# A float32 decoder block on one core: attention's gate products, the w_out loads and two operand sums placed anew

## The chip, the cores and the metric

The kernel runs on one core of a Trainium2 chip. The time of a kernel is the device time of one execution in microseconds (us). The kernel before took 751.6 us (median of three runs, 751.37 to 751.66). The engines are named as the profile does: PE (TensorE, matrix products), PEld (its weight loads), DVE (VectorE), ACT (ScalarE), POOL (GpSimd), SP (the engine that issues most transfers).

## The reference

One layer of a decoder, 1024 tokens with 16 meta tokens ahead of them, model width 1024. Everything is float32.

```python
h = rmsnorm(x, norm_g)
u_pool, z_pool, q, k, v, z_attn, f_logit, g_pool, g_attn = split(h @ w_in)
y_pool = causal_multiscale_pool(u_pool, pool_w, pool_scale) * silu(z_pool)   # 4 groups, windows 2, 4, 8, 16
log_f  = log_sigmoid(f_logit + b_forget)
y_attn = forgetting_attention(q, k, v, log_f) * silu(z_attn)                  # 8 heads of 64, causal softmax
merged = sigmoid(g_pool) * (y_pool @ w_up_pool) + sigmoid(g_attn) * (y_attn @ w_up_attn)
out    = rmsnorm(x + merged @ w_out, final_norm_g)                            # meta tokens dropped
```

## The kernel before, in words

**Split operands.** Each float32 operand of a product is rounded to a high part by ACT (for example `whi`, `yh`, line 133 or 727) and a low part is formed as the difference (`wlo`, `yl`, `oph`, `opy`). A product is then three matrix products: high by high, high by low, low by high (`g_mm3`, line 140). The low part of a w_in weight is made by POOL in four pieces of 256 columns (`pool_tt`, line 117, called at line 134); that of the pooling branch (`yl`, line 728) is made by POOL too; those of the up-projection's weights (line 811), of attention's output (line 760) and of the last product's operands (line 914) are made by DVE.

**The stages.** Norm and first projections; attention with the other projections filled in between (to about 502 us); then the part that the change touches:

1. *The za projections* (four weights, `left[0]` to `left[3]`, 502 to 575 us). `za[p]` is silu of a projection (line 741). Between them stand the pooling branch's group maps (`pooled(g)`, line 800, 12 matrix products for two groups), the normalisation of attention's output (`attn_norm`, line 748) and the gate, `Y[p] = Y[p] * za[p]` (`attn_gate`, line 750). `half_raw` runs a projection's first half and one matrix product of its second; `run` does the rest. For p = 0 and 1 the gate runs on POOL in eight pieces, for p = 2 and 3 on DVE.
2. *Sixteen up-projections* (`up`, line 819, 5.6 us each, 575.55 to 665.08). The order is the list `steps` (line 943). Each takes a raw weight (`rawu`) and a gate row (`rl`) from SP's queue. Attention's output is wanted from the fifth on. Step n of the loop (line 946) also issues a load of one block row of w_out (`w_load`, line 894) from n = 4 to 11, and with each second one the first sums on it (`t_first`, line 923, on POOL).
3. *The output product* by seven products of half size, 10.9 us each (`prod`, line 985), from sums of blocks: with G the merged branches and W = w_out, S1 = G21 + G22, S2 = S1 - G11, S3 = G11 - G21, S4 = G12 - S2, and T1 to T4 of W in the same way. They are computed in place, so S2 lies in G11, S4 in G12, T4 in W21. `prep(n)` rounds and splits the operand pair of product n, one ahead of the product. The operand sets lie in two buffers, `opy` for even n and `oph` for odd n. The operands are, in turn, (G11, W11), (G12, W21), (S2, T2), (S1, T1), (S3, T3), (S4, W22), (G22, T4). P6 in the title of the change is the product of S2 and T2, the third.

PE's order is written out by hand. On the other engines a scheduler orders the instructions by its own model of time, with the program's order as a start; `after(ins, prev)` (line 100) makes it place `ins` behind `prev` without a semaphore. Each engine and each queue then runs in that order. A buffer of the tag `b` (gate rows, za, the pooling branch) is handed on in the order in which it is let go in the program.

Of the kernel before, what the change touches and what calls it, by code (L numbers as in the profile page):

```python
# [11 lines left out]
ALU = mybir.AluOpType  # L12
# [31 lines left out]
def r32(ap):  # L44
    return ap.bitcast(F32)
# [7 lines left out]
def tile_hybrid_block(ctx, tc, x, meta, norm_g, w_in, b_forget, pool_w, pool_scale,  # L53
                      w_up_pool, w_up_attn, w_out, final_g, out):
    nc = tc.nc
# [44 lines left out]
    def after(ins, prev):  # L100
        tc.add_manual_dep(ins.ins, prev.ins.name,
                          mybir.DependencyInfo(mybir.DependencyClass.NoSync, mybir.DependencyReason.DATA),
                          reason="order")

    def rstd_of(ss):
        n = ss.shape[0]
        r = sm.tile([128, 1], F32, name="rstd", bufs=4)
        nc.vector.tensor_scalar(r[:n], ss, EPS, None, op0=ALU.add)
        nc.gpsimd.tensor_tensor(r[:n], r[:n], epsp[:n], op=ALU.pow)
        return r  # L110
# [6 lines left out]
    def pool_tt(out, x, y, op):  # L117
        for c in range(0, out.shape[-1], 256):
            ins = nc.gpsimd.tensor_tensor(out[:, c:c + 256], x[:, c:c + 256], y[:, c:c + 256], op=op)  # L119
        return ins  # L120

    def flat(t):
        return t.rearrange("p k c -> p (k c)")

    def split_w(srcs, pool=None, tags=("wh", "wl")):
        raw = wp.tile([128, KO, 128], F32, name="raw")
        k0 = 0
        for s in srcs:
            nc.sync.dma_start(raw[:, k0:k0 + s.shape[1], :], s)
            k0 += s.shape[1]  # L130
        hi = (pool or wp).tile([128, KO, 128], F32R, name="whi", tag=tags[0])
        lo = (pool or wp).tile([128, KO, 128], F32R, name="wlo", tag=tags[1])
        nc.scalar.activation(hi, raw, AF.Copy)  # L133
        pool_tt(flat(lo), flat(raw), flat(r32(hi)), ALU.subtract)
        return hi, lo

    def w_chunk(col, **kw):
# [16 lines left out]
    def run(g):  # L154
        for _ in g:
            pass
# [52 lines left out]
    QA, KA, QL, V, VT, Y = {}, {}, {}, {}, {}, {}  # L209
# [538 lines left out]
        nc.vector.tensor_tensor(Y[p], Y[p], rc, op=ALU.mult)  # L748

    def attn_gate(p):  # L750
        if p < 2:
            pool_tt(Y[p], Y[p], za[p], ALU.mult)
        else:
            nc.vector.tensor_tensor(Y[p], Y[p], za[p], op=ALU.mult)

    def attn_out(p):
        yh = hq.tile([128, SEQ], F32R, name="yah", tag="h")
# [32 lines left out]
    zp, za = [], {}  # L790
# [73 lines left out]
    attn_norm(1)  # L864
    run(left[1])
    pooled(3)
    attn_gate(0)
    pool_split(1)
    pool_chain(0)
    attn_norm(2)  # L870
    attn_norm(3)
    half_raw(left[2])
    attn_gate(1)
    run(left[2])
    pooled(2)
    pool_split(0)
    ws, rows_ = {}, {}
    ws[0, 0] = up_weights(0, 0)
    half_raw(left[3])
    attn_gate(2)  # L880
    pooled(1)
    pooled(0)
    run(left[3])
    HX.close()
# [6 lines left out]
    W = {}  # L891
    T_ = (slice(0, 512), slice(512, 1024))

    def w_load(k):
        W[k] = hq.tile([128, D], F32, name="W", tag="w")
        after(nc.sync.dma_start(W[k], wout[:, k, :]), muls[-1])

    def tt(out, x, y, op, eng):
        if eng is nc.gpsimd:
            pool_tt(out, x, y, op)  # L900
        else:
            eng.tensor_tensor(out, x, y, op=op)
# [5 lines left out]
    def pick(op_, k, n):  # L908
        return op_[n][k // 2][:, k % 2, :]

    def split_op(op_, k, src):
        h_ = pick(op_, k, 0)
        nc.scalar.activation(h_, src, AF.Copy)
        nc.vector.tensor_tensor(pick(op_, k, 1), src, r32(h_), op=ALU.subtract)  # L914
# [12 lines left out]
    def t_second(k):  # L927
        tt(side(W, k, "11"), side(W, k, "22"), side(W, k, "12"), ALU.subtract, nc.gpsimd)

    def t_third(k):  # L930
        tt(side(W, k, "21"), side(W, k, "21"), side(W, k, "11"), ALU.subtract, nc.gpsimd)

    def s_first(k):
        tt(X3[k // 2][:, k % 2, :], side(G, k, "11"), side(G, k, "21"), ALU.subtract, nc.gpsimd)

    def s_second(k):
        tt(side(G, k, "21"), side(G, k, "21"), side(G, k, "22"), ALU.add, nc.vector)
        tt(side(G, k, "11"), side(G, k, "21"), side(G, k, "11"), ALU.subtract, nc.vector)

    def s_third(k):  # L940
        tt(side(G, k, "12"), side(G, k, "12"), side(G, k, "11"), ALU.subtract, nc.gpsimd)

    steps = [(0, 0), (1, 0), (2, 0), (3, 0), (0, 1)]
    for j in range(1, 8):
# [1 line left out]
    for n, s in enumerate(steps):  # L946
        for m, fn, d in ((n + 1, up_weights, ws), (n + 2, gate_row, rows_)):
            if m < len(steps) and steps[m] not in d:
                d[steps[m]] = fn(*steps[m])
        nxt = ws[steps[n + 1]][2] if n + 1 < len(steps) else None  # L950
        up(*s, ws.pop(s), rows_.pop(s), nxt)
        if n == 0:
            for p in range(4):
                attn_out(p)
        if 4 <= n < 12:
            w_load((0, 4, 1, 5, 2, 6, 3, 7)[n - 4])
            if n % 2:
                t_first((n - 4) // 2)
        j, a = s
        if a and j < 4:  # L960
            s_first(j)
        if s == (7, 0):
            opA, opB = operand("y"), operand("y")
        if a and j >= 4:
            if j < 6:
                for k in (2 * j - 8, 2 * j - 7):
                    split_op(opA, k, side(G, k, "11"))
                    split_op(opB, k, side(W, k, "11"))
                    t_second(k)
            if j == 5:  # L970
                s_second(0)
            if j > 4:
                s_second(j - 4)
    fgb = gp.tile([128, D], F32, name="fgb", tag="g")
    nc.scalar.dma_start(fgb, bass.AP(tensor=final_g.tensor, offset=final_g.offset, ap=[[0, 128], [1, D]]))
# [53 lines left out]
    ops = {0: (opA, opB)}  # L1029

    def prep(n):
        A_, B_ = operand("yh"[n % 2]), operand("yh"[n % 2])
        sa, sb = srcs[n]
        for k in range(4):
            split_op(A_, k, side(G, k, sa) if sa else X3[k // 2][:, k % 2, :])
            split_op(B_, k, side(W, k, sb) if sb else Y3[k // 2][:, k % 2, :])
            if n == 2:
                s_third(k)
                t_third(k)
        ops[n] = A_, B_  # L1040

    lo_, hi_ = HALVES[0][0], HALVES[1][0]
    for n in range(7):
        if n < 6:
            prep(n + 1)
# [57 lines left out]
```

## Time and profile before

| | before |
|---|---|
| median of three runs | 751.6 us |
| the profiled execution | 751.64 us, span 749.9 us |
| PE busy | 733.9 us (98%) |
| DVE, ACT, POOL busy | 71%, 50%, 45% |
| mean granted PE clock | 0.992 |
| length of the up-projections | 89.53 us |
| seven products of the end | 10.92 us each but the second, 12.45 us |

How to read it: a busy PE alone decides the time, so waits of PE are looked for, and stretches in which the same number of matrix products takes longer than elsewhere. Start to start, a matrix product of 512 columns takes some 0.23 us.

### The profile page before, as it was taken

Reading aid. Unit: us, or ns where it says so; the run is one execution under the profiler, and the core shown is the slowest. Engines: PE = TensorE matmul, PEld = TensorE weight load, DVE = VectorE, ACT = ScalarE, POOL = GpSimd, SP = SyncE. Lnnn points to the kernel's source line nnn. Section 1 sums busy time; section 2 is a strip of 40 time slices with the busy share of each in tenths; the row PEclk is TensorE's granted clock in tenths of the full one; section 3 lists DMA queues with packets and bytes.
Section 4 is the critical chain, followed back from the end, with each engine's and each line's share of the span. In section 5 each row is a group of like instructions: output and inputs, shape, how many; then the busy total and the mean of one; then the engine's idle time right before and its main releaser. Section 6 shows DMA issues by size and latency. Waiting matters only on the chain.

```text
span 749.9 us, 10627 instructions
## 1 busy us (share of the span) xinstructions
PE 733.9 (98%) x3686; PEld 624.5 (83%) x3686; DVE 531.7 (71%) x989; ACT 376.7 (50%) x736; POOL 341.1 (45%) x398
## 2 busy tenths in 40 slices
PE   8999999999999999999999999999979999999996
PEld 5997999988888898888988888888867888887885
DVE  5653667768779787698697777883483554999875
ACT  6652466446557554665664455532534423524455
POOL 4331336456416545544464363354295033747243
PEclk9999999999999999999999999999998999999998
DMA  9311132221221222221224232248446167460005
GB/s 309 77 28 30 29 95 76 73 85 51 79 58 50 79 64 70 81 64 42 79 65 108 72 104 65 79 129 286 127 114 241 54 199 260 139 229 1 1 0 225
DMA packets 76424, 75.35 MB, mean 100 GB/s; under 512 B 9665, under 2 KB 60865, under 8 KB 76370
## 3 DMA queue, kind: packets, MB, share of 16 engines
q1 hardware_dynamic: 74496, 69.95, 30.4%
q10 hardware_dynamic: 1874, 4.72, 1.9%
q8 instruction: 29, 0.48, 0.3%
q14 instruction: 25, 0.20, 0.1%
HBM read 55.58 MB, written 19.07 MB: 100 GB/s over the span
## 4 chain that ended last, share of the span: by engine, by line
PE 87%; DVE 4%; POOL 2%; ACT 1%; issue 1%; POOLq 0%; ACTq 0%
PE pj L145 66%; PE pj L989 8%; PE po L626 5%; PE ps L566 3%; PE ps L565 2%; PE pt L989 2%; POOL y L119 1%; PE pj L479 1%; DVE S L605 1%; DVE pl L610 0%; PE pj L272 0%; DVE ka L259 0%; DVE oph L914 0%; DVE m L581 0%; DVE mx L590 0%
## 5 line engine op out<-in xcount | busy, mean ns | idle before, releaser
L119 POOL TENSOR_TENSOR wlo<-raw,whi 128x256 fp32r<-128x256 f32 x148 | 120.3, 844 | 191.2 <-ACT whi L133 102.7
L145 PE MATMUL pj<-hh,wlo 128*128 128x512 f32 (+4 forms) x768 | 176.2, 361 | 4.3 <-POOL wlo L119 4.3
L145 PE MATMUL pj<-hh,whi 128*128 128x512 f32 (+4 forms) x768 | 178.7, 361 | 0.7 <-ACT hh L194 0.3
L145 PE MATMUL pj<-hl,whi 128*128 128x512 f32 (+4 forms) x768 | 177.2, 359 | 0.0
L145 PEld LDWEIGHTS pj<-hh,wlo 128*128 128x128 f32 x768 | 133.3, 189 | 23.2 <-POOL wlo L119 4.9
L145 PEld LDWEIGHTS pj<-hh,whi 128*128 128x128 f32 x768 | 131.6, 188 | 18.8 <-ACT hh L194 0.5
L145 PEld LDWEIGHTS pj<-hl,whi 128*128 128x128 f32 x768 | 131.6, 188 | 17.7
L610 DVE TENSOR_TENSOR pl<-S,ph 128x512 fp32r<-128x512 f32 (+4 forms) x112 | 86.6, 788 | 19.0 <-ACT ph L609 18.5
L618 POOL TENSOR_TENSOR acc<-acc,S 128x272 f32<-128x272 f32 (+4 forms) x80 | 76.3, 954 | 9.8 <-ACT S L606 4.6
L574 ACT ACTIVATE S<-ps,negc 128x400 f32<-128x400 f32 (+2 forms) x96 | 49.2, 514 | 44.6 <-DVE S L572 35.8
L606 ACT ACTIVATE S<-S 128x512 f32<-128x512 f32 (+4 forms) x112 | 49.5, 478 | 32.8 <-DVE S L605 32.6
L609 ACT ACTIVATE ph<-S 128x512 fp32r<-128x512 f32 (+4 forms) x112 | 52.2, 480 | 15.8 <-PE po L626 14.6
L581 DVE TENSOR_TENSOR m<-m,S 128x272 f32<-128x272 f32 (+4 forms) x80 | 41.4, 517 | 23.8 <-ACT S L574 22.1
L133 ACT ACTIVATE whi<-raw 128x1024 fp32r<-128x1024 f32 x37 | 39.1, 1057 | 32.2 <-PE pj L145 27.8
L605 DVE TENSOR_TENSOR S<-S,pt 128x512 f32<-128x512 f32 (+4 forms) x112 | 51.9, 498 | 0.8
L832 DVE TENSOR_TENSOR rl<-pj,rl 128x512 f32<-128x512 f32 x32 | 22.0, 689 | 29.1 <-PE pj L145 28.0
L572 DVE SCALAR_TENSOR_TENSOR S<-ps,negc,mask 128x128 f32<-128x128 f32 (+2 forms) x72 | 23.7, 330 | 22.9 <-PE ps L566 22.7
L310 ACT ACTIVATE st<-pj 128x512 f32<-128x512 f32 x40 | 23.7, 592 | 29.0 <-PE pj L145 19.6
L626 PE MATMUL po<-pl,V 128*128 128x512 f32 (+4 forms) x112 | 37.6, 336 | 0.0
L566 PE MATMUL ps<-ql,ka 128*128 128x512 f32 (+4 forms) x112 | 37.5, 334 | 0.0
L565 PE MATMUL ps<-qa,ka 128*128 128x512 f32 (+4 forms) x112 | 35.9, 321 | 0.5 <-ACT S L574 0.5
L989 PE MATMUL pj<-opy 128*128 128x512 f32 (+1 forms) x168 | 36.3, 375 | 0.0
(187 smaller groups left out, 1144.9 us busy)
## 6 DMA issues: line engine op xcount, KB each, us to landing
raw<-in_w_in_dram SPq DMA_DIRECT2D x40, 512.0 KB, 3.9
sp_gp<-st SPq DMA_DIRECT2D x16, 256.0 KB, 2.0
sp_ga<-st SPq DMA_DIRECT2D x16, 256.0 KB, 2.0
rl<-sp_gp SPq DMA_DIRECT2D x8, 512.0 KB, 5.3
rl<-sp_ga SPq DMA_DIRECT2D x8, 512.0 KB, 4.7
W<-in_w_out_dram SPq DMA_DIRECT2D x8, 512.0 KB, 5.7
xr<-in_x_dram SPq DMA_DIRECT2D x8, 512.0 KB, 4.2
xt<-in_x_dram SPq DMA_DIRECT2D x7, 512.0 KB, 7.9
```

Source lines behind the costliest of these rows:

```text
L119: ins = nc.gpsimd.tensor_tensor(out[:, c:c + 256], x[:, c:c + 256], y[:, c:c + 256], op=op)
L145: nc.tensor.matmul(ps, a, b, start=(i == 0), stop=(i == len(seq) - 1))
L565: nc.tensor.matmul(ps[:kb, c0:], ka[:, k0:k0 + kb], qa[:, q0 + c0:q0 + 512], start=True, stop=False)
L566: nc.tensor.matmul(ps[:kb, c0:], ka[:, k0:k0 + kb], ql[:, q0 + c0:q0 + 512], start=False, stop=True)
L574: nc.scalar.activation(s[:kb, f0:], ps[:kb, f0:], AF.Identity, bias=nb_)
L605: nc.vector.tensor_tensor(s[:kb, c0:], s[:kb, c0:], self.pm[:kb, c0:], op=ALU.subtract)
L606: exps.append(nc.scalar.activation(s[:kb, c0:], s[:kb, c0:], AF.Exp))
L609: nc.scalar.activation(ph[:kb, c0:], s[:kb, c0:], AF.Copy)
L610: dves.append(nc.vector.tensor_tensor(pl[:kb, c0:], s[:kb, c0:], r32(ph[:kb, c0:]), op=ALU.subtract))
L618: nc.gpsimd.tensor_tensor(acc[:kb, c0:], acc[:kb, c0:], s[:kb, c0:], op=ALU.add)
L626: nc.tensor.matmul(self.po[:, c0:], v, r[:kb, c0:], start=(b == 0 and i == 0), stop=(b == self.nb - 1 and i == 1))
L989: nc.tensor.matmul(ps, pick(A_, k, p)[:, i * 128:(i + 1) * 128], pick(B_, k, q)[:, c0:c1], start=start and n == 0, stop=n == 11, skip_grou ...
```

## The change

Three edits, and one small one.

- All four gate products of attention run on DVE, each as one operation over 1024 columns. For p = 0, 1 and 2 they stand behind the last w_in weight's low part in the scheduler's order (`los[-1]`), and in the program behind the first half of the last za projection.
- The w_out loads and the first sums on them start at step 2 of the up-projections in place of step 4.
- S4 and T4 (`s_third`, `t_third`) move from the third operand set's `prep` to the fourth's, go piece by piece in turn, and each piece waits by a semaphore (`behind`) for the last low part of the third set.
- `s_second` of block row 3 (its S1 and S2) moves from the loop of the up-projections to the start of the third set's `prep`.

```diff
+    def behind(ins, prev):
+        tc.add_manual_dep(ins.ins, prev.ins.name,
+                          mybir.DependencyInfo(mybir.DependencyClass.Sync, mybir.DependencyReason.DATA),
+                          reason="wait")
...
-        pool_tt(flat(lo), flat(raw), flat(r32(hi)), ALU.subtract)
+        los.append(pool_tt(flat(lo), flat(raw), flat(r32(hi)), ALU.subtract))
...
     def attn_gate(p):
-        if p < 2:
-            pool_tt(Y[p], Y[p], za[p], ALU.mult)
-        else:
-            nc.vector.tensor_tensor(Y[p], Y[p], za[p], op=ALU.mult)
+        after(nc.vector.tensor_tensor(Y[p], Y[p], za[p], op=ALU.mult), los[-1])
...
     pooled(3)
-    attn_gate(0)
     pool_split(1)
...
     half_raw(left[2])
-    attn_gate(1)
     run(left[2])
...
     half_raw(left[3])
+    attn_gate(0)
+    attn_gate(1)
+    pooled(1)
     attn_gate(2)
-    pooled(1)
     pooled(0)
...
-    def s_third(k):
-        tt(side(G, k, "12"), side(G, k, "12"), side(G, k, "11"), ALU.subtract, nc.gpsimd)
+    def s_third(k, prev):
+        for c in range(0, 512, 256):
+            g12, g11 = [side(G, k, b)[:, c:c + 256] for b in ("12", "11")]
+            ins = nc.gpsimd.tensor_tensor(g12, g12, g11, op=ALU.subtract)
+            behind(ins, prev)
+            w21, w11 = [side(W, k, b)[:, c:c + 256] for b in ("21", "11")]
+            behind(nc.gpsimd.tensor_tensor(w21, w21, w11, op=ALU.subtract), prev)
...
-        if 4 <= n < 12:
-            w_load((0, 4, 1, 5, 2, 6, 3, 7)[n - 4])
+        if 2 <= n < 10:
+            w_load((0, 4, 1, 5, 2, 6, 3, 7)[n - 2])
             if n % 2:
-                t_first((n - 4) // 2)
+                t_first((n - 2) // 2)
...
-            if j > 4:
+            if 4 < j < 7:
                 s_second(j - 4)
...
         sa, sb = srcs[n]
+        if n == 2:
+            s_second(3)
         for k in range(4):
             split_op(A_, k, side(G, k, sa) if sa else X3[k // 2][:, k % 2, :])
-            split_op(B_, k, side(W, k, sb) if sb else Y3[k // 2][:, k % 2, :])
-            if n == 2:
-                s_third(k)
-                t_third(k)
+            lows[n] = split_op(B_, k, side(W, k, sb) if sb else Y3[k // 2][:, k % 2, :])
+            if n == 3:
+                s_third(k, lows[2])
```

On POOL around the last za weight, before (`wlo`: a weight's low part, `yl`: the pooling branch's low part, `y<-y,za`: the gate; x4 means four pieces):

```order
L618 TENSOR_TENSOR acc<-acc,S 128x16
L119 TENSOR_TENSOR wlo<-raw,whi 128x256 x16
L119 TENSOR_TENSOR yl<-rl,yh 128x256 x4
L119 TENSOR_TENSOR y<-y,za 128x256 x8
L119 TENSOR_TENSOR wlo<-raw,whi 128x256 x4
L119 TENSOR_TENSOR yl<-rl,yh 128x256 x12
```

The same place with the change:

```order
L625 TENSOR_TENSOR acc<-acc,S 128x16
L124 TENSOR_TENSOR wlo<-raw,whi 128x256 x16
L124 TENSOR_TENSOR yl<-rl,yh 128x256 x4
L124 TENSOR_TENSOR wlo<-raw,whi 128x256 x4
L124 TENSOR_TENSOR yl<-rl,yh 128x256 x12
```

The eight pieces of the gate are gone from ahead of the last weight's four pieces. They come back on DVE, where the same place reads, before (`rl<-pj,psc,rl`: the pooling branch's scale product, `pll`: a low part of the pooled rows) and after:

```order
L748 TENSOR_TENSOR y<-y,rc 128x1024
L726 SCALAR_TENSOR_TENSOR rl<-pj,psc,rl 128x512 x2
L785 TENSOR_TENSOR pll<-u,plh 128x1024
L748 TENSOR_TENSOR y<-y,rc 128x1024
L754 TENSOR_TENSOR y<-y,za 128x1024
L726 SCALAR_TENSOR_TENSOR rl<-pj,psc,rl 128x512 x4
```

```order
L755 TENSOR_TENSOR y<-y,rc 128x1024
L733 SCALAR_TENSOR_TENSOR rl<-pj,psc,rl 128x512 x2
L789 TENSOR_TENSOR pll<-u,plh 128x1024
L755 TENSOR_TENSOR y<-y,rc 128x1024
L758 TENSOR_TENSOR y<-y,za 128x1024 x3
L733 SCALAR_TENSOR_TENSOR rl<-pj,psc,rl 128x512 x4
```

One gate has become three, ahead of the four scale products of groups 1 and 0. On DVE at the first of the seven products, before (`oph`: low parts of the second operand set, `G<-G`: S1 and S2, `xr<-pj`: a result added to the residual):

```order
L914 TENSOR_TENSOR oph<-G,oph 128x512
L834 TENSOR_TENSOR G<-rl 128x512
L914 TENSOR_TENSOR oph<-W,oph 128x512
L902 TENSOR_TENSOR G<-G 128x512
L914 TENSOR_TENSOR oph<-G,oph 128x512
L902 TENSOR_TENSOR G<-G 128x512
L914 TENSOR_TENSOR oph<-W,oph 128x512
L914 TENSOR_TENSOR oph<-G,oph 128x512 x2
L914 TENSOR_TENSOR oph<-W,oph 128x512 x2
L995 TENSOR_TENSOR xr<-pj,xr 128x512 x3
```

With the change:

```order
L918 TENSOR_TENSOR oph<-G,oph 128x512
L838 TENSOR_TENSOR G<-rl 128x512
L918 TENSOR_TENSOR oph<-W,oph 128x512
L918 TENSOR_TENSOR oph<-G,oph 128x512
L918 TENSOR_TENSOR oph<-W,oph 128x512
L918 TENSOR_TENSOR oph<-G,oph 128x512 x2
L918 TENSOR_TENSOR oph<-W,oph 128x512 x2
L1001 TENSOR_TENSOR xr<-pj,xr 128x512 x2
L906 TENSOR_TENSOR G<-G 128x512 x2
L1001 TENSOR_TENSOR xr<-pj,xr 128x512
```

S1 and S2 of block row 3 now stand behind all low parts of the second operand set and two of the residual adds. On POOL the pieces of S4 and T4 now alternate, and nine of the sixteen stand among the first two rows' gains (`xr<-xr,fgb`) and behind them.

More of the change, by code (lines that the diff above doesn't have):

```diff
@@ L120, in pool_tt @@
         return ins
+    los = []
     def flat(t):
@@ L913, in split_op @@
         nc.scalar.activation(h_, src, AF.Copy)
-        nc.vector.tensor_tensor(pick(op_, k, 1), src, r32(h_), op=ALU.subtract)
+        return nc.vector.tensor_tensor(pick(op_, k, 1), src, r32(h_), op=ALU.subtract)
     X3 = [gp.tile([128, 2, 512], F32, name="X3", tag="g") for _ in range(2)]
@@ L928, in t_second @@
         tt(side(W, k, "11"), side(W, k, "22"), side(W, k, "12"), ALU.subtract, nc.gpsimd)
-    def t_third(k):
-        tt(side(W, k, "21"), side(W, k, "21"), side(W, k, "11"), ALU.subtract, nc.gpsimd)
     def s_first(k):
@@ L1028, in tile_hybrid_block @@
     srcs = [("11", "11"), ("12", "21"), ("11", "11"), ("21", "12"), (None, None), ("12", "22"), ("22", "21")]
-    ops = {0: (opA, opB)}
+    ops, lows = {0: (opA, opB)}, {}
     def prep(n):
```

## The prediction

> **What bounds the kernel now.** I read the chain of waits first: 87% of it is PE. From 502.71 on, it leaves PE in two places only.
>
> ```profile
> 502.71 48.98 PE pj L145 x212
> 551.70 10.51 POOL y L119 x8
> 562.21 0.69 POOL wlo L119
> 562.94 102.30 PE pj L145 x428
> ...
> 676.58 2.38 DVE oph L914 x2
> ```
>
> A change here pays only by what it does to PE at these two places. The sum of waits of PE from 440 us to the end has just these two rows (us in total, times, longest):
>
> ```profile
> PE pj L145 <- POOL wlo L119: 4.3, 1, 4.3
> PE pj L989 <- DVE oph L914: 0.9, 2, 0.6
> ```
>
> A wait is not yet a price, so I read stretches next. The columns are length; PE, weight load, DVE, ACT and POOL busy (instructions); granted PE clock; DMA share; GB/s.
>
> ```profile
> 542.27:553.37 11.10, 11.10 (x49) 9.02 (x48) 11.03 (x10) 3.96 (x5) 8.31 (x6) 1.00 0.87 221
> 554.76:575.55 20.79, 16.46 (x62) 12.86 (x61) 8.36 (x9) 5.35 (x9) 18.56 (x23) 0.84 0.44 155
> 558.44:562.94 4.50, 0.17 (x1) 0.00 (x1) 1.82 (x2) 0.00 (x0) 4.50 (x6) 0.80 0.00 0
> 562.94:568.11 5.17, 5.17 (x13) 4.03 (x13) 0.00 (x0) 0.60 (x1) 4.76 (x7) 0.51 0.34 105
> ...
> 665.08:676.00 10.92, 10.92 (x49) 9.01 (x48) 10.88 (x13) 4.12 (x9) 7.88 (x7) 1.00 0.53 192
> 676.00:688.45 12.45, 11.50 (x50) 8.93 (x49) 12.45 (x16) 3.11 (x6) 9.58 (x10) 1.00 0.00 1
> 688.45:699.37 10.92, 10.92 (x50) 9.01 (x48) 9.56 (x15) 7.96 (x19) 9.51 (x12) 1.00 0.00 0
> ```
>
> The first wait costs more than its 4.3 us: behind it the granted clock is 0.51 for 5.17 us. The second costs more than its 0.9: that product takes 12.45 us, its neighbours 10.92.
>
> **Term 1: the four gate products off POOL.** PE and POOL at the wait, from the timeline:
>
> ```profile
> 551.52 2.02 PE L145 MATMUL pj<-hh,wlo 128*128 128x512 f32 x8
> ...
> 556.59 2.02 PE L145 MATMUL pj<-hl,whi 128*128 128x512 f32 x8
> ...
> 562.94 3.78 PE L145 MATMUL pj<-hh,wlo 128*128 128x512 f32 x8 [4.33 <-POOL wlo L119]
> ...
> 530.06 3.83 POOL L119 TENSOR_TENSOR wlo<-raw,whi 128x256 fp32r<-128x256 f32 x4 [8.29 <-ACT whi L133]
> ...
> 551.66 10.54 POOL L119 TENSOR_TENSOR y<-y,za 128x256 f32<-128x256 f32 x8
> 562.17 2.77 POOL L119 TENSOR_TENSOR wlo<-raw,whi 128x256 fp32r<-128x256 f32 x4
> ```
>
> The last za weight's low part (wlo, four pieces) stands behind the eight y pieces; PE starts when the first piece is done (562.17 + 0.7). The program gives PE 60 matmuls between 554.76 and 575.55: 24 for the first half, 1, then 12 for pooling groups 1 and 0, then 23. At the pitch of the undisturbed stretch (48 in 11.10 us, 0.2313 each) they need 13.9 us, not 20.8. So the stall costs **6.9 us**: 4.5 of gap, and some 2.4 of half speed (5.17 us for what needs 12 pitches, 2.8).
>
> The Trainium skill (TensorE: Matmul & The Clock Gate, "What's actually happening") puts the time at half clock after idling at about 3.4 us of sustained work, which would cost 1.7; with that the sum below would be 0.7 smaller. The row has 5.17 us, so the row stands.
>
> With the y pieces gone, when does wlo come? Its buffer is let go when PE is through with the previous low part (551.52 + 2.02 = 553.5; the same step a weight earlier began at 530.06). At that earlier row's pace, 3.83 for four, it is ready at 557.5. PE wants the pieces from 558.5 on, one each 0.46 us. Their slow bound is the y pieces' median, next row (ns: least, median, most):
>
> ```profile
> L119 POOL TENSOR_TENSOR y<-y,za x8: 717/1706/1792, 551.7 to 561.5; 128x256 f32<-128x256 f32 x8
> ```
>
> Four at 1.71 end at 560.4, where PE wants the last at 559.9: 0.5 late. I take zero, since DVE works from PSUM or waits in part of that stretch.
>
> **What DVE pays.** The rows behind the wait:
>
> ```profile
> 558.53 1.74 DVE L754 TENSOR_TENSOR y<-y,za 128x1024 f32<-128x1024 f32 x1
> ...
> 568.31 2.85 DVE L726 SCALAR_TENSOR_TENSOR rl<-pj,psc,rl 128x512 f32<-128x512 f32 x4 [8.04 <-PE pj L145]
> ...
> 569.15 2.67 ACT L727 ACTIVATE yh<-rl 128x512 fp32r<-128x512 f32 x4 [1.79 <-DVE rl L726]
> ...
> 564.90 2.80 POOL L119 TENSOR_TENSOR yl<-rl,yh 128x256 fp32r<-128x256 f32 x4
> 569.86 5.62 POOL L119 TENSOR_TENSOR yl<-rl,yh 128x256 fp32r<-128x256 f32 x8 [2.16 <-ACT yh L727]
> ```
>
> DVE gets two more products of 1.74. They fall into its 8.04 us of idling, but PE now comes 6.9 us sooner, so that idle time shrinks to almost nothing. Queued behind the gates are the four scale products of groups 1 and 0 (L726); behind those ACT's yh and POOL's eight yl pieces, for which the first up-projection waits. This is what is late next. PE finishes group 1's first half at 554.76 + 28 x 0.2313 = 561.2; the gates end at 558.53 + 3 x 1.74 = 563.8; the four scale products take to 566.6; ACT's first yh is there at 565.1 (0.7 for the scale product, 2.67 / 4 for the rounding). POOL has by then done group 2's four yl pieces beside the gates (557.5 + 4 x 1.71 = 564.3), and its sixth of the next eight, the last piece PE needs, is done at 565.1 + 6 x 0.70 = 569.3. PE wants it at 554.76 + 64 x 0.2313 = 569.6. A margin of 0.3 is no margin; bounds: 0, and with wlo at its slow bound 560.4 + 4 x 1.71 + 6 x 0.70 = 571.4, so 1.8 late. I take **0.3 us** lost. A gap that short keeps the clock: in the product with the two short waits it stayed 1.00.
>
> **Term 2: w_out two projections sooner.** POOL waits for it; PE never does:
>
> ```profile
> L896 SPq DMA_DIRECT2D W<-in_w_out_dram x8: 420/440/504, 599.9 to 640.6; - x8
> ...
> DMA W<-in_w_out_dram: 17.6, 3
> ...
> DMA to landing us min/median/max: 3.7/5.7/6.8
> ...
> 575.55:597.95 22.40, 22.40 (x98) 17.99 (x97) 12.92 (x16) 12.11 (x15) 0.00 (x0) 1.00 0.33 103
> ...
> 605.75 1.44 POOL L119 TENSOR_TENSOR X<-G 128x256 f32<-128x256 f32 x2 [30.27 <-DVE G L834]
> ...
> rl<-sp_gp SPq DMA_DIRECT2D x8, 512.0 KB, 5.3
> ```
>
> Eight loads move by two steps of 5.6 us (four in 22.40), and the first POOL sums behind them fall into the 30 us in which POOL idles. On SP each pushes what stands behind it by its 0.44 us of issue, against steps of 5.6. **Zero**. Without that cover a raw weight or gate row would be late by one landing, 5.7 us. What it brings is fewer POOL pieces beside DVE later. SP also gets a new wait: the second gate row now takes a buffer that group 2's yl pieces free (564.3, at worst 567.3). With 5.3 us to land it is there by 572.6 at worst, and step 1 first multiplies it near 577 (568.7 + 5.6 + 2.8). Also zero.
>
> **Term 3: S4 and T4 behind the low parts.** DVE and POOL ahead of the 12.45 us product:
>
> ```profile
> 667.35 0.68 DVE L914 TENSOR_TENSOR oph<-G,oph 128x512 fp32r<-128x512 f32 x1
> ...
> 669.71 1.22 DVE L902 TENSOR_TENSOR G<-G 128x512 f32<-128x512 f32 x1
> ...
> 672.00 1.22 DVE L902 TENSOR_TENSOR G<-G 128x512 f32<-128x512 f32 x1
> ...
> 676.58 2.37 DVE L914 TENSOR_TENSOR oph<-W,oph 128x512 fp32r<-128x512 f32 x2
> ...
> 668.12 2.27 POOL L119 TENSOR_TENSOR G<-G 128x256 f32<-128x256 f32 x2 [9.51 <-DVE oph L914]
> ...
> 680.89 4.69 POOL L119 TENSOR_TENSOR W<-W 128x256 f32<-128x256 f32 x4
> ...
> 691.20 0.65 POOL L1012 TENSOR_SCALAR sst<-sso 128x1 f32<-128x1 f32 x1
> 691.92 2.27 POOL L119 TENSOR_TENSOR xr<-xr,fgb 128x256 f32<-128x256 f32 x2
> ```
>
> From 668.12, when POOL's sums begin, a DVE operation of that shape takes 1.22 instead of 0.68, and the last low parts end at 678.95. The change takes away both causes: sums S1 and S2 of block 3 (L902, twice 1.22) leave this queue, and POOL waits. Eight low parts and one G sum at 0.68 from 667.35 end at 673.5, before PE starts the product at 676.0; at 1.22 each they would end at 678.3, 0.7 after PE wants the last (676.0 + 7 x 0.228, from 10.92 / 48). So the product falls to its neighbours' 10.92: **1.5 us** gained.
>
> The new wait: POOL stands until the second set's low parts are done, 676.0 + 8 x 0.68 = 681.4. Queued behind the waiting sum are 16 pieces and the row gains; no one waits for the gains before the sixth product. G12 is wanted for the sixth product's operands when the fourth is nearly through, 708.8 (699.37 + 10.92 - 1.5). 16 pieces at 1.17 (4.69 / 4) and two gains of 2.9 end at 706. The fifth product's eight low parts, all at 1.22 beside POOL and with four adds of 0.68, would take from 697.4 to 709.9, where PE wants the last of them at 708.8 + 1.6 = 710.4. Zero, slow bound 0.5.
>
> **Sum.** -6.9 - 1.5 + 0.3 = -8.1. The profiled execution took 751.64 us (span 749.9), the median is 751.6, so both bases agree: **743.5 us**, span about 741.8. Bounds: no loss at all, 743.2; all slow bounds (0.5 + 1.8 + 0.5), 746.0. With 0.5 for pitch below and 0.2 above (the runs lie 0.3 apart), the range is 742.7 to 746.2.
>
> **Rivals.**
> 1. *Late yl pieces.* DVE's gates hold the pooling low parts, PE waits 1 to 2.5 us at the first up-projection: 744.5 to 746. For it: the margin of 0.3. Against: the 2.85 and 5.62 rows show that scale products and yl pieces run side by side at full speed. 0.14.
> 2. *The product keeps its wait, or hands it on.* The low parts stay late, or the sums moved back meet the fourth and fifth operand sets: 743.5 + 1.5 = 745.0. For it: the POOL work is the same, only later. Against: 2.5 us to spare, and at 1.22 throughout only 0.7 is lost. 0.10.
> 3. *Slower: POOL starved by DVE.* From 553.5, POOL has 14 pieces up to the one the first up-projection needs (4 wlo, 4 + 4 + 2 yl). If all ran at the 1.71 of the y pieces they would end at 577.4, 7.8 late; that is longer than the gap that halved the clock, so 2.4 comes on top: 743.2 + 10.2 = 753.4. It decides from 1.58 a piece on (6.0 late + 2.4 = 8.4); from 1.47 to 1.65 the gain is eaten to within 0.2%. Against: pieces run at 0.70 when DVE idles or reads PSUM, and DVE has only some six long two-input operations there. 0.04 slower, 0.05 no change.
>
> The Trainium skill (GPSIMD Engine Reference, "Key points") speaks for rival 3: GpSimd shares its SBUF interfaces with VectorE and is slowed by VectorE instructions with two SBUF inputs, which all gates are. The trace agrees in the 717/1706 ns row, but not for every piece.
>
> **How the numbers follow.** Forecast 0.66 (742.7 to 744.4), rival 1 0.14, rival 2 0.10, rival 3 0.09, something else 0.01. The range takes in all but the last two. A measurement of this kernel tells 0.2% (1.5 us) from no change: faster 0.91, same 0.05, slower 0.04.
>
> **What would show it.** Right: no PE wait for wlo near 558, no stretch at clock 0.5 there, up-projections starting near 568.7 and not 575.55; all seven products at 10.9; POOL's sums starting only after the second set's low parts. Rival 1: a PE wait for yl near 569. Rival 2: a PE wait for an oph or opy low part. Wrong altogether: the last wlo piece still after 560, or the up-projections starting at 575.

## The result and the profile after

The changed kernel takes **743.91 us** (median of four runs, 743.83 to 744.34) against 751.63 (four runs, 751.37 to 751.95). The ratio is 0.9898, 95% interval 0.9881 to 0.9915: faster by 1.0%, some 7.7 us. The forecast was 743.5, with a range from 742.7 to 746.2.

| | before | after |
|---|---|---|
| the profiled execution, its span | 751.64, 749.9 | 743.96, 742.2 |
| start of the last za projection | 554.76 | 555.23 |
| from there to the first up-projection | 20.79 | 13.86 |
| sixteen up-projections | 89.53 | 89.79 |
| second product (the others 10.92 to 10.94) | 12.45 | 10.94 |
| PE, DVE, POOL busy | 98%, 71%, 45% | 99%, 72%, 45% |
| mean granted PE clock | 0.992 | 0.997 |

The rows add up: -6.93 for the stretch with the wait, -1.51 for the product, +0.26 for the up-projections, and +0.47 that had gathered before the first changed instruction, together -7.71.

From 503.18 us on, the chain of waits of the changed kernel no longer leaves PE until the last product is through (724.62 + 11.09 = 735.71 us); its first rows:

```profile
503.18 155.86 PE pj L152 x669
659.04 8.20 PE pj L995 x36
667.24 2.72 PE pt L995 x12
669.97 8.21 PE pj L995 x36
```

The 669 operations of the first row are one run without a break; before, a chain of POOL's gate pieces cut it. The sum of waits of PE from 440 us on, which had two rows before, is empty.

The stretches of the changed kernel (length; PE, weight load, DVE, ACT and POOL busy, instructions; granted PE clock; DMA share; GB/s):

```profile
555.23:569.09 13.86, 13.86 (x62) 11.27 (x60) 11.75 (x11) 5.24 (x9) 12.99 (x12) 1.00 0.35 129
569.09:571.12 2.03, 2.03 (x9) 1.42 (x8) 1.78 (x2) 1.81 (x2) 2.03 (x3) 1.00 1.01 408
569.09:658.88 89.79, 89.79 (x385) 71.87 (x384) 59.66 (x80) 35.31 (x47) 31.86 (x36) 1.00 0.57 197
658.88:669.80 10.92, 10.92 (x49) 9.01 (x48) 9.98 (x17) 4.01 (x9) 0.00 (x0) 1.00 0.41 150
669.80:680.74 10.94, 10.94 (x49) 9.01 (x48) 7.47 (x13) 6.33 (x15) 5.69 (x9) 1.00 0.00 0
```

In the first stretch PE is busy throughout at a clock of 1.00, where it had been 16.46 of 20.79 at 0.84. In the fourth, the first product, POOL does nothing (7.88 us of work before); in the fifth the wait for the low parts is gone.

PE, then POOL, of the changed kernel, each in order of time, at the place of the old wait and behind it:

```profile
569.09 1.10 PE L152 MATMUL pj<-yh,whu 128*128 128x512 f32 x4
570.08 1.20 PE L152 MATMUL pj<-yl,whu 128*128 128x512 f32 x4
571.12 1.09 PE L152 MATMUL pj<-yh,wlu 128*128 128x512 f32 x4
...
554.14 4.08 POOL L124 TENSOR_TENSOR wlo<-raw,whi 128x256 fp32r<-128x256 f32 x4 [1.81 <-ACT whi L140]
558.19 6.76 POOL L124 TENSOR_TENSOR yl<-rl,yh 128x256 fp32r<-128x256 f32 x4
565.81 7.05 POOL L124 TENSOR_TENSOR yl<-rl,yh 128x256 fp32r<-128x256 f32 x8 [0.87 <-ACT yh L734]
...
674.89 0.75 POOL L944 TENSOR_TENSOR G<-G 128x256 f32<-128x256 f32 x1 [25.61 <-DVE opy L918]
...
692.86 1.19 POOL L947 TENSOR_TENSOR W<-W 128x256 f32<-128x256 f32 x1
```

And DVE of the changed kernel at the same places:

```profile
559.23 5.12 DVE L758 TENSOR_TENSOR y<-y,za 128x1024 f32<-128x1024 f32 x3
564.27 2.71 DVE L733 SCALAR_TENSOR_TENSOR rl<-pj,psc,rl 128x512 f32<-128x512 f32 x4
...
659.78 0.68 DVE L918 TENSOR_TENSOR oph<-G,oph 128x512 fp32r<-128x512 f32 x1
...
663.99 1.29 DVE L918 TENSOR_TENSOR oph<-W,oph 128x512 fp32r<-128x512 f32 x2
...
697.47 1.83 DVE L918 TENSOR_TENSOR opy<-Y,opy 128x512 fp32r<-128x512 f32 x2
```

The wlo pieces are done at 558.22, ahead of PE (558.91). The first group of yl pieces beside the gates takes 1.69 each (6.76 / 4), the second 0.88. PE gets the first eight products of its first up-projection a little later than its pitch (0.23) asks: 2.03 us from 569.09 to 571.12 where eight pitches are 1.85. The second product's low parts, which had ended at 678.95, 2.95 us into that product, now end at 665.28, 4.5 us before it. POOL's sums begin when POOL has stood idle for 25.6 us, and are done at 694.05.

### The profile page after: what moved, and what is told of

It reads as the page before. It is cut to its first block, busy times and chain, and to the rows that moved or that the text cites. A ratio compares the mean times of both kernels' runs of the same rounds, so it can differ in the third digit from the quotient of the medians.

```text
span 742.2 us, 10619 instructions
## 1 busy us (share of the span) xinstructions
PE 731.2 (99%) x3686; PEld 622.7 (84%) x3686; DVE 533.2 (72%) x991; ACT 377.0 (51%) x736; POOL 332.8 (45%) x390
## 4 chain that ended last, share of the span: by engine, by line
PE 87%; DVE 5%; ACT 1%; issue 1%; POOLq 0%; POOL 0%; ACTq 0%
PE pj L152 65%; PE pj L995 8%; PE po L633 5%; PE ps L573 2%; PE ps L572 2%; PE pt L995 2%; PE pj L486 1%; DVE S L612 1%; DVE pl L617 1%; DVE ka L266 0%; PE pj L279 0%; DVE pt L603 0%; ACT S L581 0%; DVE mt L593 0%; ACT whi L140 0%
## 5 line engine op out<-in xcount | busy, mean ns | idle before, releaser
L152 PE MATMUL pj<-hh,wlo 128*128 128x512 f32 (+4 forms) x768 | 174.4, 358 | 0.0
```

What stands on the lines that cost most here:

```text
L152: nc.tensor.matmul(ps, a, b, start=(i == 0), stop=(i == len(seq) - 1))
```

## The experiments

All twelve compute the whole output. The last column but one is the length of the stretch from the last za projection's start to the first up-projection; 13.86 is that stretch without loss.

| kernel | median us | ratio to before | stretch | up-projections | second product |
|---|---|---|---|---|---|
| the change | 743.91 | 0.9898 (0.9881 to 0.9915) | 13.86 | 89.79 | 10.94 |
| e1 gates alone | 745.59 | 0.9912 (0.9897 to 0.9927) | 13.86 | 89.85 | 12.45 |
| e2 loads alone | 750.50 | 0.9979 (0.9970 to 0.9988) | 20.20 | 89.53 | 11.10 |
| e3 sums alone | 750.50 | 0.9982 (0.9973 to 0.9991) | 20.04 | 89.53 | 10.94 |
| e4 change without loads | 744.81 | 0.9900 (0.9887 to 0.9914) | 13.86 | 89.72 | 10.94 |
| e5 S1, S2 moved, S4, T4 as before | 744.25 | 0.9889 (0.9874 to 0.9903) | 13.86 | 89.74 | 10.94 |
| e6 S4, T4 moved, S1, S2 as before | 744.23 | 0.9889 (0.9874 to 0.9904) | 13.86 | 89.84 | 10.94 |
| e7 one gate left on POOL, ahead | 749.42 | 0.9958 (0.9943 to 0.9972) | 19.28 | 89.53 | 10.94 |
| e8 two gates on POOL, behind | 748.39 | 0.9948 (0.9931 to 0.9965) | 13.87 | 93.77 | 10.94 |
| e9 gates behind the scale products | 745.26 | 0.9909 (0.9895 to 0.9923) | 13.87 | 90.79 | 10.94 |
| e10 before, one more product on POOL | 753.43 | 1.0015 (1.0005 to 1.0024) | 21.62 | 89.54 | 12.44 |
| e11 gates, S1 and S2 moved, no more | 744.52 | 0.9895 (0.9881 to 0.9910) | 13.86 | 90.41 | 10.93 |
| e12 gates behind the last yl | 744.02 | 0.9889 (0.9873 to 0.9906) | 13.86 | 89.53 | 10.94 |

The start of the last za projection lay between 554.76 and 555.99 us in these profiled executions, though PE's work ahead of it is the same in all. But for 0.4 us in the change and in e12, the differences are there after the first 52 us and do not grow from there on. So a total tells nothing under about 1.2 us, and what is smaller is read by stage.

**e1. The gates alone, on the kernel before.**

```diff
     def attn_gate(p):
-        if p < 2:
-            pool_tt(Y[p], Y[p], za[p], ALU.mult)
-        else:
-            nc.vector.tensor_tensor(Y[p], Y[p], za[p], op=ALU.mult)
+        after(nc.vector.tensor_tensor(Y[p], Y[p], za[p], op=ALU.mult), los[-1])
```

and the calls stand as in the change.

> The kernel before with the gate products' move alone. If the prediction's terms are right and add up: 751.6 - 6.9 + 0.3 = 745.0 us, no PE wait for wlo, up-projections starting some 6.5 us sooner, the second product still 12.4 us long. Rival (the terms overlap: the sums' stall was partly a consequence of the first stall, as the clock or DVE's backlog came from it): the second product is at 10.9 here too, 743.5.

It took 745.59 against 752.13. The stretch has 13.86, the second product still 12.45. The wait of PE that is left is the old one of the product:

```profile
PE pj L988 <- DVE oph L913: 0.9, 2, 0.6
```

The first and the third term do not touch each other. The gates give 6.5 of the 7.7 us.

**e2. The loads alone.**

```diff
-        if 4 <= n < 12:
-            w_load((0, 4, 1, 5, 2, 6, 3, 7)[n - 4])
+        if 2 <= n < 10:
+            w_load((0, 4, 1, 5, 2, 6, 3, 7)[n - 2])
             if n % 2:
-                t_first((n - 4) // 2)
+                t_first((n - 2) // 2)
```

> The kernel before with the w_out loads and their first sums two steps sooner, nothing else. Prediction's term: zero, 751.6, both PE waits as before. Rival: POOL's earlier sums free DVE ahead of the second product, so that its low parts come in time and some of the 1.5 us is gained by the loads: 750.1 to 751.3, second product shorter than 12.4.

The forecast of no effect is wrong. The product falls from 12.45 to 11.10, and the ratio lies below 1 with its whole interval (0.9970 to 0.9988). POOL in order of time in the kernel before:

```profile
645.20 4.12 POOL L119 TENSOR_TENSOR W<-W 128x256 f32<-128x256 f32 x4 [3.97 <-DVE opy L914]
649.28 2.33 POOL L119 TENSOR_TENSOR Y<-W 128x256 f32<-128x256 f32 x2
651.58 7.02 POOL L119 TENSOR_TENSOR W<-W 128x256 f32<-128x256 f32 x6
```

POOL in e2, which lies 0.2 us later there:

```profile
645.40 4.13 POOL L119 TENSOR_TENSOR W<-W 128x256 f32<-128x256 f32 x4 [3.97 <-DVE opy L914]
650.16 2.32 POOL L119 TENSOR_TENSOR W<-W 128x256 f32<-128x256 f32 x2 [0.63 <-DVE opy L914]
653.80 1.88 POOL L119 TENSOR_TENSOR W<-W 128x256 f32<-128x256 f32 x2 [1.32 <-DVE opy L914]
```

Before, twelve pieces run without a break from 645.20 to 658.60. The four of the last block row's first sums are done some 14 us sooner in e2, so eight are left, with breaks. DVE in e2, at the operands of the second product:

```profile
666.18 0.68 DVE L914 TENSOR_TENSOR oph<-G,oph 128x512 fp32r<-128x512 f32 x1
...
675.43 2.38 DVE L914 TENSOR_TENSOR oph<-W,oph 128x512 fp32r<-128x512 f32 x2
```

DVE has next to no idle time between 645.7 and 680 in the kernel before, so what it loses beside POOL at 650 it still owes at 667. Up to the first low part DVE does the same operations in both kernels (from 645.68 to 667.35 before, from 645.88 to 666.18 in e2); eight of them take 1.22 or more before and five in e2, and the way is 1.37 us shorter. The first low part began 2.27 us after the first product's start before (667.35 against 665.08), and 0.90 after it in e2 (666.18 against 665.28). From there on e2's operations are as slow as before, 1.22 each. The backlog is enough by itself for 1.35 of the 1.53 us.

**e3. The sums alone** (S1 and S2 of block row 3 moved, S4 and T4 with their wait).

```diff
-            if j > 4:
+            if 4 < j < 7:
                 s_second(j - 4)
...
+        if n == 2:
+            s_second(3)
...
-            if n == 2:
-                s_third(k)
-                t_third(k)
+            lows[n] = split_op(B_, k, side(W, k, sb) if sb else Y3[k // 2][:, k % 2, :])
+            if n == 3:
+                s_third(k, lows[2])
```

> The kernel before with S4 and T4 behind the low parts and S1, S2 of block row 3 moved, nothing else. Prediction's term: 751.6 - 1.5 = 750.1, all seven products at 10.9, the wait for wlo as before (4.3 us and the half clock behind it). Rival: the sums moved back cost a wait in a later product, 751 or more.

The product takes 10.94, and the wait for wlo is untouched. DVE in e3:

```profile
667.27 0.68 DVE L919 TENSOR_TENSOR oph<-G,oph 128x512 fp32r<-128x512 f32 x1
...
671.48 1.29 DVE L919 TENSOR_TENSOR oph<-W,oph 128x512 fp32r<-128x512 f32 x2
```

It begins as late as before (667.27) and runs at 0.68: the last low part ends at 672.77, where the prediction had 673.5.

**e4. The change without the loads.**

```diff
-        if 2 <= n < 10:
-            w_load((0, 4, 1, 5, 2, 6, 3, 7)[n - 2])
+        if 4 <= n < 12:
+            w_load((0, 4, 1, 5, 2, 6, 3, 7)[n - 4])
             if n % 2:
-                t_first((n - 2) // 2)
+                t_first((n - 4) // 2)
```

> The changed kernel with the w_out loads back at step 4. Prediction's term: zero, the same 743.9 as the change, all seven products at 10.9. Rival: without the sooner loads POOL's sums still run beside DVE's low parts at the end of the up-projections, and the second product waits again: 744.3 to 745.4.

744.81, product 10.94, no wait of PE. With the sums in place, the loads bring nothing that these runs can tell.

**e5 and e6. One half of the sums' edit each,** with gates and loads as in the change. e5 leaves S4 and T4 where they were, e6 leaves S1 and S2. The edit of e5:

```diff
+            if n == 2:
+                s_third(k)
+                t_third(k)
-            if n == 3:
-                s_third(k, lows[2])
```

> The change with S4 and T4 as before (no semaphore, in the third set's preparation): of the two edits to the sums only S1, S2 of block row 3 are moved. By the prediction's working (nine DVE operations at 1.22 end 0.7 us after PE wants the last) a short wait of up to 0.7 us stays in the second product: 743.9 to 744.6. Rival: POOL's pieces beside DVE are the whole cause, the second product stays near 12.4, 745.4.

The edit of e6:

```diff
-            if 4 < j < 7:
+            if j > 4:
                 s_second(j - 4)
...
-        if n == 2:
-            s_second(3)
```

> The change with S1, S2 of block row 3 left in the loop of the up-projections: of the two edits to the sums only the wait of S4 and T4. Eleven DVE operations at 0.68 from 667.35 (scale of the trace of before) end at 674.8, before the product starts at 676.0: no wait, 743.9. Rival: the two sums in that queue are what makes the low parts late, then a wait stays and it takes 744.5 to 745.4.

Both have 10.94 and no wait of PE (744.25 and 744.23); the wait of up to 0.7 that was expected of e5 did not come. With the loads in, either half is enough.

**e11. Gates and the move of S1 and S2, and no more.** On the change, the loads and S4, T4 stand as before; the edits are those of e4 and e5 together.

> The gates' move as in the change, the w_out loads at step 4 and S4, T4 as in the kernel before; of the sums only S1, S2 of block row 3 are moved. It measures what that edit does without the help of the loads. By the prediction's working nine DVE operations at 1.15 to 1.22 start to start end 0.1 to 0.7 us after PE wants the last: second product 11.0 to 11.6 (12.45 before, 10.94 in the change). Rival: without the loads it stays at 12.45, or is 10.94 because the last low part is wanted later than worked out.

The second product has 10.93 here too (11.0 to 11.6 was expected), with low parts that all but the first run beside POOL. DVE in e11:

```profile
662.25 0.68 DVE L913 TENSOR_TENSOR oph<-G,oph 128x512 fp32r<-128x512 f32 x1
...
669.18 2.37 DVE L913 TENSOR_TENSOR oph<-W,oph 128x512 fp32r<-128x512 f32 x2
```

Its first product starts at 659.98, so the low parts start as late as before (2.27 us into it) and end 11.57 into it. PE wants the last one 12.5 into it (10.92 and seven pitches of 0.228). That one sum puts the runs in order. Its first column of numbers is the end of the last low part, counted from the first product's start:

| kernel | last low part ends | late by (12.5 subtracted) | second product |
|---|---|---|---|
| before | 13.87 | 1.4 | 12.45 |
| e2 loads alone | 12.53 | 0.0 | 11.10 |
| e11 S1, S2 moved | 11.57 | in time by 0.9 | 10.93 |
| e5 loads, S1, S2 moved | 10.16 | in time by 2.3 | 10.94 |
| e12, below: S4, T4 moved | 8.98 | in time by 3.5 | 10.94 |
| e3, e4, e6 | 7.6 to 7.7 | in time by 4.8 or more | 10.94 |
| the change | 6.40 | in time by 6.1 | 10.94 |

Three remedies each bring the low parts forward, the loads by 1.3, S1 and S2 by 2.3, the wait of S4 and T4 by 4.9 (by 6.1 with S1 and S2, in e3), and 1.4 was all that was missing.

**e7. One gate left on POOL ahead of the last weight's low part.**

```diff
     def attn_gate(p):
-        after(nc.vector.tensor_tensor(Y[p], Y[p], za[p], op=ALU.mult), los[-1])
+        if p == 0:
+            pool_tt(Y[p], Y[p], za[p], ALU.mult)
+        else:
+            after(nc.vector.tensor_tensor(Y[p], Y[p], za[p], op=ALU.mult), los[-1])
```

and its call stands behind `pooled(3)` again.

> The change with one of the four gates back on POOL ahead of the last weight's low part: four pieces in place of eight (before) or none (the change). They end near 558.5 and the first wlo piece near 559.7, 1.2 us after PE wants it. Theory (a short gap does not lower the clock): the gap alone, about 1.2 us, clock 1.00 behind it, 744.7 to 745.5. Rival (each gap brings the slow clock): 2.4 us on top, 747 to 748.

It took 749.42, above both forecasts, and the stretch 19.28: with half of POOL's gate pieces gone, most of the loss is still there. The waits of PE in e7 (us in total, times, longest):

```profile
PE pj L152 <- POOL wlo L124: 2.8, 3, 0.9
```

POOL, DVE and PE in e7:

```profile
558.59 5.72 POOL L124 TENSOR_TENSOR wlo<-raw,whi 128x256 fp32r<-128x256 f32 x4
...
559.63 3.40 DVE L761 TENSOR_TENSOR y<-y,za 128x1024 f32<-128x1024 f32 x2
...
560.34 0.73 PE L152 MATMUL pj<-hh,wlo 128*128 128x512 f32 x2 [0.94 <-POOL wlo L124]
562.01 0.73 PE L152 MATMUL pj<-hh,wlo 128*128 128x512 f32 x2 [0.94 <-POOL wlo L124]
563.67 1.45 PE L152 MATMUL pj<-hh,wlo 128*128 128x512 f32 x4 [0.93 <-POOL wlo L124]
```

And its stretches:

```profile
560.34:564.93 4.59, 2.72 (x9) 1.38 (x9) 2.69 (x2) 0.00 (x0) 4.59 (x4) 1.00 0.00 0
564.93:568.33 3.40, 3.40 (x9) 2.64 (x8) 0.93 (x2) 1.21 (x2) 2.14 (x4) 0.50 0.86 269
```

The four wlo pieces start at 558.59 (554.14 in the change), where at 0.7 each PE would hardly wait, but now DVE's last normalisation product and two gates run beside them, and the first three take some 1.7 us each. PE waits for each of these three, 0.9 us at a time. The clock is still 1.00 for 1.26 us behind the third gap and then 0.50 for 3.40 us. Of the loss of 5.42 (19.28 - 13.86), the slow clock is 1.55 (eight products in 3.40 us where eight pitches are 1.85); the other 3.9 go to the three gaps, counted from start to start, and to the four products behind the third. So three short gaps cost about as much clock as the one gap of 4.59 us in e3 (below: eight products in 3.28 us, 1.4 lost), and to take away half of POOL's gate pieces brings back 1.5 of the 6.93 us.

**e8. Gates 0 and 1 on POOL, behind the last wlo:** the place is the change's, the engine before's.

```diff
     def attn_gate(p):
-        after(nc.vector.tensor_tensor(Y[p], Y[p], za[p], op=ALU.mult), los[-1])
+        if p < 2:
+            for c in range(0, SEQ, 256):
+                after(nc.gpsimd.tensor_tensor(Y[p][:, c:c + 256], Y[p][:, c:c + 256], za[p][:, c:c + 256],
+                                              op=ALU.mult), los[-1])
+        else:
+            after(nc.vector.tensor_tensor(Y[p], Y[p], za[p], op=ALU.mult), los[-1])
```

> The change with gates 0 and 1 on POOL again, but behind the last weight's low part. Theory (the pooling low parts are next in line, DVE was needed for the gates): eight pieces more ahead of the yl pieces, 558.2 + 2 x 1.7 + 6 x 0.72 = 565.9, then ten yl pieces at 0.72 to 573.1 or later, PE waits 3 us or more at the first up-projection: 747 without a slow clock, 749.5 with one. Rival (only the place ahead of wlo mattered): 743.9.

748.39: the stretch is mended (13.87), and the up-projections take 93.77 in place of 89.79. Waits and stretches of e8:

```profile
PE pj L152 <- POOL yl L124: 2.6, 1, 2.6
```

```profile
572.74:576.02 3.28, 3.28 (x9) 2.61 (x10) 3.01 (x2) 1.33 (x2) 1.33 (x2) 0.56 0.42 164
```

The eight gate pieces now stand ahead of the yl pieces, PE waits 2.63 us for these, and the granted clock is 0.56 over the next 3.28 us. To move the gates off the place ahead of wlo is not enough. A place on POOL behind the yl pieces was not tried.

**e9. The gates on DVE, behind the scale products of groups 1 and 0.** The forecast's +0.3 came from gates that hold those scale products up. (`scales` collects the scale products.)

```diff
-        after(nc.vector.tensor_tensor(Y[p], Y[p], za[p], op=ALU.mult), los[-1])
+        after(nc.vector.tensor_tensor(Y[p], Y[p], za[p], op=ALU.mult), scales[-1])
...
     half_raw(left[3])
+    pooled(1)
+    pooled(0)
     attn_gate(0)
     attn_gate(1)
-    pooled(1)
     attn_gate(2)
-    pooled(0)
```

> The change with the first three gates behind the scale products of pooling groups 1 and 0 on DVE, so that the yl pieces start some 2 us sooner. Theory (the first up-projection takes 5.8 us in the change where others take 5.6, as it waits piece by piece for yl): the first up-projection falls to 5.6, 0.2 to 0.3 us gained, 743.6. Rival: the gates now hold attention's output parts or the next weight's low part: 743.9 or more.

It got worse, not better: up-projections 90.79. POOL and DVE in e9, and its wait of PE:

```profile
564.10 10.00 POOL L124 TENSOR_TENSOR yl<-rl,yh 128x256 fp32r<-128x256 f32 x8 [1.53 <-ACT yh L735]
...
565.29 4.69 DVE L759 TENSOR_TENSOR y<-y,za 128x1024 f32<-128x1024 f32 x3
```

```profile
PE pj L152 <- POOL yl L124: 0.9, 1, 0.9
```

Counted from the start of the last za projection (555.88 here), the last eight yl pieces start 2.4 us sooner than in the change, and then run beside the gates at 1.25 each (10.00 / 8) and end 0.6 later. What holds the first up-projection is as much the contention as the queue.

**e12. The gates on DVE behind the last yl piece, by a semaphore,** with the loads and S1, S2 as before (S4 and T4 with their wait). `yls` collects the yl pieces; the three calls behind `half_raw(left[3])` go.

```diff
-        after(nc.vector.tensor_tensor(Y[p], Y[p], za[p], op=ALU.mult), los[-1])
+        behind(nc.vector.tensor_tensor(Y[p], Y[p], za[p], op=ALU.mult), yls[-1])
...
-    attn_gate(3)
+    for p in range(4):
+        attn_gate(p)
```

> All four gates on DVE, but behind the pooling branch's last low part by a semaphore, so that no gate runs beside the yl pieces; of the other edits only the wait of S4 and T4 (loads at step 4, S1, S2 in the loop). Theory: the yl pieces run at 0.7 each and are there before PE asks, the up-projections take 89.53 in place of 89.79; the second product 10.94, as eleven DVE operations at 0.68 end before it starts: 743.6. Rivals: the later gates hold attention's output or a weight's split and an up-projection waits (over 744); the wait alone is not enough without the loads (second product above 11).

POOL and DVE in e12:

```profile
564.18 5.64 POOL L124 TENSOR_TENSOR yl<-rl,yh 128x256 fp32r<-128x256 f32 x8 [1.55 <-ACT yh L734]
...
569.86 3.50 DVE L758 TENSOR_TENSOR y<-y,za 128x1024 f32<-128x1024 f32 x3 [4.39 <-POOL yl L124]
```

Kept apart, both are faster: a yl piece takes 0.70 (5.64 / 8) and a gate 1.17 (3.50 / 3, against 1.71 in the change). The up-projections have their 89.53 again, so the 0.26 is recovered, and every stage of e12 is without loss. Its median (744.02, ratio 0.9889) can't be told from the change's. It needs one remedy for the product, not three.

**e10. A longer stall,** to see what the drop of the clock costs: on the kernel before, one product of the normalisation (`Y[1] * rc`) moves to POOL too.

```diff
-        nc.vector.tensor_tensor(Y[p], Y[p], rc, op=ALU.mult)
+        if p == 1:
+            pool_tt(Y[p], Y[p], rc, ALU.mult)
+        else:
+            nc.vector.tensor_tensor(Y[p], Y[p], rc, op=ALU.mult)
```

> The kernel before with the normalisation of one of the rows of attention's output on POOL too: twelve pieces ahead of wlo in place of eight, so a longer gap. Theory (the slow clock behind a long gap lasts a fixed time): gap 4.5 + 3 to 5 us, the stretch at half clock again about 5 us, price of it again 2.4, time 751.6 + 3 to 5 = 754.6 to 756.6. Rival (the slow stretch grows with the gap): half clock for 8 to 10 us, 756 to 759.

753.43, ratio 1.0015 (1.0005 to 1.0024). POOL and PE in e10:

```profile
556.12 2.82 POOL L119 TENSOR_TENSOR y<-y,rc 128x256 f32<-128x256 f32 x4
...
565.36 3.52 PE L145 MATMUL pj<-hh,wlo 128*128 128x512 f32 x8 [6.09 <-POOL wlo L119]
```

```profile
565.36:568.71 3.35, 3.35 (x8) 2.62 (x9) 0.00 (x0) 0.00 (x0) 3.35 (x6) 0.54 0.03 8
```

Both forecasts were too high. The gap grew by 1.8 us only (6.09): with one operation less on DVE, which stood idle for 3.70 us there, POOL's pieces ran faster, these four at 0.70. The slow stretch behind it is shorter than before's, 3.35 us. e2 and e3 have before's wait unchanged; PE there, first e2 and then e3:

```profile
563.85 3.62 PE L145 MATMUL pj<-hh,wlo 128*128 128x512 f32 x8 [4.45 <-POOL wlo L119]
567.27 0.54 PE L145 MATMUL pj<-hh,whi 128*128 128x512 f32 x1
567.65 0.40 PE L145 MATMUL pj<-plh,pwh 128*128 128x512 f32 x1
```

```profile
563.91 3.44 PE L150 MATMUL pj<-hh,wlo 128*128 128x512 f32 x8 [4.59 <-POOL wlo L124]
567.19 0.39 PE L150 MATMUL pj<-hh,whi 128*128 128x512 f32 x1
```

At 0.43 a product, they are slow for 3.8 us (to 567.65) and 3.3 us (to 567.19), against 5.17 in the one profiled execution of the kernel before, with gaps of 4.45, 4.59 and 4.33. The length of the slow stretch does not follow the gap in these runs; with nearly the same gap it differs between executions.

## Why the prediction was right, and where it was not

**Term 1, the stall of 6.9 us: right.** The stretch fell by 6.93, and by as much in e1. wlo was forecast for 557.5 and is done at 558.22 in an execution that runs 0.47 late by then, so 557.75. The match to 0.03 flatters the term: forecast and result are read on the same profiled execution of the kernel before. All that was named as a sign is there: no wait for wlo, clock 1.00, up-projections from 569.09 (568.6 without the 0.47).

Its second part, 2.4 for half speed, was read from the one execution at hand and is at the upper end. Counted in the same way, as the time of the slow products less as many pitches, the same wait cost 1.7 in e2 (nine products in 3.80 us) and 1.4 in e3 (eight in 3.28). The slow stretches seen are 5.17 (before), 3.8, 3.3, 3.4 (e7), 3.3 (e8) and 3.35 (e10). The Trainium skill (TensorE: Matmul & The Clock Gate, "What's actually happening") gives about 3.4 us; the later runs, 3.3 to 3.8, lie near it, and the prediction, which let the row of 5.17 stand, took one execution for the rule. For an execution with the shorter stretch its gain was 0.6 to 0.75 too large (20.79 against 20.20 in e2 and 20.04 in e3); totals with a drift of 1.2 can't show that.

**"A gap that short keeps the clock": right where it was used, wrong as a rule.** In the change the pieces are late by 0.2 and the clock stays 1.00, and one gap of 0.92 in e9 kept it too (up-projections longer by 1.26 only). e7 shows three gaps of 0.94 within 4.3 us after which it fell to 0.50.

**What DVE pays, +0.3: right in size, by luck.** The up-projections took 0.26 longer. By the prediction's chain nothing was lost (569.3 against 569.6); the 0.3 was an allowance between bounds of 0 and 1.8. The chain held up to the yl pieces, with the 0.47 taken off: the gates end at 563.88 (forecast 563.8), the scale products at 566.5 (566.6). The margin is thin, as was said: with the same order at this place, the up-projections took 89.72 in e4, where the last eight yl pieces start 10.49 us after the last za projection does, 89.79 in the change (10.58) and 90.41 in e11 (10.78), there with a wait of 0.55. That is Rival 1 in small (it had 1 to 2.5 us); 0.2 us kept it out of the change. What the step had left out is that the eight yl pieces can meet DVE's next operations, so that they took 0.88 each in place of 0.70; e9 and e12 show that contention from both sides.

**Term 2, zero for the loads: right in the change, wrong by itself.** The prediction saw the mechanism ("fewer POOL pieces beside DVE later") and put no price on it. e2 shows the price, 1.35 us of the product. In the change nothing of it is left, since the same 1.5 us can be gained only once (e4). The step that failed is the search for the cause of the 12.45: it looked at DVE's operations from 668.12 on, beside POOL's sums there, and not at those that had made the queue late by 2.3 us before. The late start at 667.35 was taken as given.

**Term 3, 1.5 us: right in size,** and its cause only half told. 1.51 measured; POOL's sums began 5.1 us into the second product (forecast 5.4) and ended 24.3 into it (forecast 30), and the fifth product's low parts were done at 699.30, 3.3 us before it, so the slow bound of 0.5 did not come. Here the prediction was careful without need: ten of POOL's sixteen pieces ran at some 0.74, not 1.17; beside these DVE was for the most part idle or reading PSUM.

Wrong was the estimate for the case that POOL keeps contending, "at 1.22 each they would end at 678.3, 0.7 after PE wants the last". e11 is that case, and PE does not wait. The durations of a row overlap: at 1.22 long, the operations start every 1.15 (2.37 for two), and the first two took 0.60. That makes 9.30 us from first to last, so 676.65 on before's clock, a microsecond early. So the move of S1 and S2 alone would have done.

**Rival 3, POOL starved by DVE,** did not decide, but is real: four pieces at 1.69 beside the gates in the change, while the twelve others up to the first up-projection took 0.88 to 1.02 on the mean. e7 is the place where it bites. The Trainium skill (GPSIMD Engine Reference, "Key points") names the shared interfaces; the trace adds that both sides pay, DVE's gate 1.71 beside POOL and 1.17 alone.

Settled only in part is where the 0.47 us ahead of the change comes from: 0.07 is there after 52 us, the rest is gathered in the attention stage between 349 and 397 us. Ahead of that, two DVE operations in the same place of the same order took 2.56 us (from 332.04) in place of 1.27; e12 has the same step (2.57), the other runs have not. What brings it on is open, and it is not put down to the change.

## What to carry to other kernels

When an in-order engine has no idle time for tens of microseconds, ask of a late operation not only what slows it down but since when its queue is late; work that is moved off a neighbour 15 us earlier can mend the wait as well as work moved off the spot. Price a PE stall of some microseconds as its gap and a slow-clock stretch that varies between executions, and do not count several short gaps as free of the clock's price: in e7 they were not. Where two engines slow each other down, as POOL and DVE do when both read two tensors from SBUF, put them one behind the other by a real wait: in e12 both got faster.

## What the runs showed of the hardware that was not expected

- The granted clock fell to 0.50 after three gaps of 0.94 us within 4.3 us (e7), and to 0.56 after one of 2.63 (e8), and stayed at 1.00 after one gap of 0.92 (e9).
- The slow stretch lasted 3.3 to 5.2 us, with no visible relation to a gap of 2.6 to 6.1 us.
- Beside a run of twelve yl pieces on POOL, which kept their 0.70 each, one DVE operation of 512 columns took 5.35; the same one took 0.69 to 1.29 in the other runs. POOL and DVE in e8:

```profile
565.73 8.34 POOL L124 TENSOR_TENSOR yl<-rl,yh 128x256 fp32r<-128x256 f32 x12
...
569.26 5.35 DVE L820 TENSOR_TENSOR wlu<-rawu,whu 128x512 fp32r<-128x512 f32 x1 [4.63 <-DMA rl<-sp_gp]
```

Elsewhere the two engines share the loss (POOL 1.69 and DVE 1.71 in the change); here only DVE was slow. Why is open.
